# The two mix stages in written order: one stretch of attention per round, one share of dense products behind it

## The chip, the core and the metric

The kernel runs on one core of a Trainium2 chip. The metric is the device time of one execution in microseconds: the median of several runs. Beside it there is one execution that was taken with the hardware profiler; all rows below come from that one.

## What is computed

Two transformer blocks over 512 positions of width 1024, in fp32. The first block has dilated, banded and stick-breaking attention and a convolutional feed-forward part; the change doesn't touch it. The second block puts 16 meta tokens ahead (528 positions) and has two layers of: feed-forward, **mix**, feed-forward. The mix is what is changed:

```python
proj = rmsnorm(h, mix_norm[l]) @ w_in[l]
rq, rk, rv, rg, dq, dk, dv = split(proj)
y_ret = retention_group(rq, rk, rv, rg, ret_gn_w[l])        # 4 heads of 128
y_diff = diff_attention_group(dq, dk, dv, ...)              # 4 heads, two maps of 64 each
h = h + concatenate([y_ret, y_diff], -1) @ w_out[l]

# differential attention, for each head and each block of queries:
s = einsum('mid,mjd->mij', qb, k) * scale                   # two maps m, causal
p = softmax(s)
o = (p[0] - lam * p[1]) @ v                                 # then rms norm of o and a factor

# retention, for each head (written out over all positions in the kernel):
o = ((q @ k.T) * decay) @ v                                 # then group norm, times silu(gate)
```

## The kernel before

All activations lie feature-major: partitions are features, columns are positions (528, the meta tokens first). A dense product W.T y is done in fp32r with both operands split into a high and a low part, H and L, so that each tile of 128 features costs three products, HH, HL and LH (`gemm_steps`, L195 to L210, all its products on L205). One **dense step** is one k of `gemm_steps`: 128 rows, three products, over two column segments of 264 (R2, all 528 positions), so six products; over R1 (512 positions, layer 1's queries and gates) three products of 512 columns. A `gemm` of 128 output features has 8 steps. Weights come in blocks of 256 output features through `wblock` (L188): two loads of 512 KB on SP's queue into `wraw` (three buffers), a high part on ScalarE (L171) and a low part on VectorE (L172) into `wqH` and `wqL` (four buffers each, so two blocks).

The kernel is written as a program order for a planner. The planner orders the instructions of each engine by priority (the place in the program) and by what it expects to be ready, so dense products of later parts can slip in where an earlier part would wait. In a region under `manual_schedule(engines={nc.tensor.engine})` TensorE keeps the order in which its instructions are written; the other engines are ordered by the planner as elsewhere. Before, the attention of the first block is under it, the mix is not.

`mix` (L1398) does for each layer, in program order: V of the four differential heads (`v_heads`, `v_major`); for two pairs of heads the projections q and k, rotated (`rotate`) and split by `stack`, and then `diff_heads`; V of the retention heads; for two pairs of heads q and k rotated and `ret_head`; the norm of the differential outputs and their transposes (`feature_major`); the gates; the norm of the retention outputs, their transposes and products with the gates; the first half of the output projection (`w_out2a`); and the second half in halves of the columns, which also prepares the next feed-forward part.

`diff_block` (L1633) handles one head and one block b of queries. Block 0 is the 16 meta tokens (layer 0 alone); blocks 1 to 4 have 128 queries and 16 + 128 b keys. It is a generator with three visits. The first does the scores of both maps, one after the other: a product over 128 rows (L1648: `stack` has put the high part of the 64 query features over the low part, against the high part of the keys twice), a product over 64 rows (L1649: high part of q, low part of k) and, on the diagonal, a mask through a bf16 product with the identity (L1651); then the maximum on VectorE (L1653), the exponential with its sum on ScalarE (L1660), and the combination of the two maps on VectorE (L1668, L1671). 528 keys are done in two spans of 264. The second visit transposes the weights of the 128-wide key blocks (L1678) and copies them (L1679). The third transposes the 16 meta columns (L1682), copies them (L1683) and does the value products (L1685; L1686 for the 16 meta rows; fp32, so two instructions for a product). `diff_heads` (L1615) calls the visits as a pipeline: scores of block i, transposes of i-1, values of i-2.

`ret_head` (L1691) does one head of retention: scores of key block j against all later queries (L1706), times the decay (L1707, into one tile `rw`), then the value products of query block i (L1715), a copy (L1717) and the statistics (L1719, L1720).

PSUM has eight buffers: four `g` (dense products), two `s` (scores, transposes of outputs), one `t` and one `o`.

## Time and profile before

| | us |
|---|---|
| median of 3 runs | 3121.83 |
| lowest, highest | 3114.48, 3124.24 |
| the profiled execution | 3116.68 |
| its span, first to last instruction | 3114.9 |
| mix of layer 0 in it | about 1425 to 1722 |
| mix of layer 1 in it | about 2456 to 2737 |

Times in the rows are microseconds from the start of the span unless a column says ns. PE is TensorE, PEld its weight loads, DVE VectorE, ACT ScalarE, POOL GpSimd, SP the engine whose queue issues the loads. The recorded end of a product is modelled and overlaps the next product; what a product takes away from the engine is read from its start to the next start.

### The profile page before, as it was taken

The page shows a single profiled execution, that of the slowest core. Times are in us where ns is not written, and L with a number is a line of the kernel's source. Part 1 is how long each engine was busy: PE and PEld are TensorE (multiplying, and loading weights), DVE is VectorE, ACT ScalarE, POOL GpSimd, SP SyncE. Part 2 cuts the span into 40 slices and gives each one's busy share as a digit, 9 for nine tenths or more (in the row PEclk, how much of TensorE's full clock was granted, in tenths as well). Part 3 has the DMA queues.
Part 4 walks back from the last instruction along what each step waited for, and adds up shares of the span by engine and source line. Part 5 has one row for each costly group of instructions (what it writes and reads, how often), then busy time and mean ns, then how long its engine had stood idle before and what let it go on. Part 6 is the DMA issues. An engine that isn't in the chain of part 4 may idle for free.

```text
span 3114.9 us, 54477 instructions
## 1 busy us (share of the span) xinstructions
PE 3071.9 (99%) x22120; PEld 2843.6 (91%) x22120; DVE 2229.0 (72%) x4185; ACT 1522.3 (49%) x2948; POOL 30.9 (1%) x64
## 2 busy tenths in 40 slices
PE   8998999999999999999999999999999999999998
PEld 6875789998989999999899999999999988899998
DVE  5253767978877887776766877768777586687775
ACT  5445556655555554444643544444444464354443
POOL 1100100000000000000000000000000000000000
PEclk9998999999999999999999999999999999999999
DMA  6221346223323322332112232322323211223232
GB/s 222 63 85 61 105 146 200 90 95 102 109 95 113 119 89 91 100 115 90 52 58 76 76 108 89 108 93 87 109 90 114 97 58 62 72 84 106 95 109 75
DMA packets 97020, 304.38 MB, mean 98 GB/s; under 512 B 12263, under 2 KB 20863, under 8 KB 96640
## 3 DMA queue, kind: packets, MB, share of 16 engines
q1 hardware_dynamic: 90448, 286.63, 27.9%
q0 software_dynamic: 2720, 7.78, 0.8%
q10 hardware_dynamic: 3600, 6.49, 0.7%
q8 instruction: 173, 2.83, 0.4%
q14 instruction: 79, 0.65, 0.1%
HBM read 290.34 MB, written 14.45 MB: 98 GB/s over the span
## 4 chain that ended last, share of the span: by engine, by line
PE 96%; DVE 1%; ACT 1%; DMA 1%; issue 1%; DVEq 0%; SPq 0%; ACTq 0%
PE ps_g L205 37%; PE ps_g L315 18%; PE ps_g L313 9%; PE ps_s L205 8%; PE ps_g L243 7%; PE ps_o L313 4%; PE ps_g L652 1%; PE ps_o L243 1%; PE ps_s L1649 1%; PE ps_s L1706 1%; PE ps_o L1685 1%; PE ps_o L1715 1%; DMA num<-in_x 1%; PE ps_o L1686 0%; PE ps_s L1648 0%
## 5 line engine op out<-in xcount | busy, mean ns | idle before, releaser
L172 DVE TENSOR_TENSOR wqL<-wraw,wqH 128x512 fp32r<-128x512 f32 (+1 forms) x672 | 604.0, 913 | 277.4 <-ACT wqH L171 269.2
L171 ACT CAST wqH<-wraw 128x512 fp32r<-128x512 f32 (+1 forms) x672 | 526.1, 799 | 511.2 <-PE ps_g L205 278.1
L205 PE MATMUL ps_g<-yH,wqH 128*128 128x264 f32 (+2 forms) x1584 | 462.5, 329 | 0.0
L205 PE MATMUL ps_g<-yL,wqH 128*128 128x264 f32 (+2 forms) x1584 | 453.4, 322 | 0.4 <-DVE yL L451 0.4
L205 PE MATMUL ps_g<-yH,wqL 128*128 128x264 f32 (+2 forms) x1584 | 452.9, 323 | 0.3 <-DVE wqL L172 0.2
L315 PE MATMUL ps_g<-t,wqH 128*128 128x264 f32 (+1 forms) x1696 | 314.7, 283 | 0.0
L205 PEld LDWEIGHTS ps_g<-yH,wqH 128*128 128x128 f32 x1584 | 275.2, 189 | 34.0 <-issue 12.2
L205 PEld LDWEIGHTS ps_g<-yL,wqH 128*128 128x128 f32 x1584 | 276.8, 189 | 21.7 <-DVE yL L451 1.1
L205 PEld LDWEIGHTS ps_g<-yH,wqL 128*128 128x128 f32 x1584 | 274.9, 189 | 23.5 <-DVE wqL L172 0.7
L315 PEld LDWEIGHTS ps_g<-t,wqH 128*128 128x128 f32 x1696 | 262.5, 188 | 1.8
L315 PE MATMUL ps_g<-t,wqL 128*128 128x264 f32 (+1 forms) x848 | 239.5, 282 | 0.0
L171 ACT CAST wqH<-ws 128x1024 fp32r<-128x1024 f32 x96 | 101.0, 1052 | 122.7 <-issue 32.7
L315 PEld LDWEIGHTS ps_g<-t,wqL 128*128 128x128 f32 x848 | 159.9, 189 | 0.0
L313 PE MATMUL ps_g<-t,wqH 128*128 128x264 f32 (+1 forms) x768 | 142.8, 283 | 0.0
L205 PE MATMUL ps_s<-hL,wqH 128*128 128x264 f32 (+1 forms) x544 | 141.3, 317 | 0.0
L205 PE MATMUL ps_g<-hL,wqH 128*128 128x264 f32 (+1 forms) x544 | 141.2, 317 | 0.0
L205 PE MATMUL ps_g<-hH,wqL 128*128 128x264 f32 (+1 forms) x544 | 141.1, 317 | 0.0
L205 PE MATMUL ps_s<-hH,wqL 128*128 128x264 f32 (+1 forms) x544 | 141.1, 317 | 0.0
L205 PE MATMUL ps_g<-hH,wqH 128*128 128x264 f32 (+1 forms) x544 | 141.0, 317 | 0.0
L205 PE MATMUL ps_s<-hH,wqH 128*128 128x264 f32 (+1 forms) x544 | 141.0, 316 | 0.0
L295 DVE TENSOR_TENSOR ws<-wraw 128x512 f32<-128x512 f32 x96 | 66.4, 692 | 82.1 <-DMA wraw<-in_ffn_w_gate 32.6
L172 DVE TENSOR_TENSOR wqL<-ws,wqH 128x1024 fp32r<-128x1024 f32 x96 | 117.3, 1222 | 5.8 <-ACT wqH L171 1.9
(451 smaller groups left out, 8046.9 us busy)
## 6 DMA issues: line engine op xcount, KB each, us to landing
wraw<-in_ffn_w_gate SPq DMA_DIRECT2D x88, 512.0 KB, 3.7
wraw<-in_ffn_w_up SPq DMA_DIRECT2D x88, 512.0 KB, 3.7
wraw<-in_ffn_w_down SPq DMA_DIRECT2D x88, 512.0 KB, 3.5
wraw<-in_w_in SPq DMA_DIRECT2D x86, 512.0 KB, 3.7
wraw<-in_w_up SPq DMA_DIRECT2D x64, 512.0 KB, 3.7
wraw<-in_w_down SPq DMA_DIRECT2D x32, 512.0 KB, 3.6
wraw<-in_w_gate SPq DMA_DIRECT2D x24, 512.0 KB, 3.8
tmp_p<-gates ACTq DMA_DIRECT2D x24, 256.0 KB, 3.3
```

Of the source, the lines that this page charges most:

```text
L171: self.nc.scalar.copy(out=H, in_=raw)
L172: self.nc.vector.tensor_sub(out=L, in0=raw, in1=H.bitcast(F32))
L205: self.nc.tensor.matmul(t[:, :m], lhsT=a, rhs=b[:, o:o + m], start=(k == 0 and i == 0), stop=(k == nk - 1 and i == 2))
L243: self.nc.tensor.matmul(q[:, :m], lhsT=a, rhs=b[:, o:o + m], start=(k == 0 and i == 0), stop=(k == nk - 1 and i == 2))
L295: nc.vector.tensor_add(out=S[:, :512], in0=A21, in1=A22)
L313: nc.tensor.matmul(ps, lhsT=a, rhs=b, start=first, stop=last)
L315: nc.tensor.matmul(ps, lhsT=a, rhs=b, start=False, stop=last, skip_group_check=True)
L652: nc.tensor.matmul(ps[:, :256], lhsT=a[:, ts], rhs=w, start=(k == 0 and i == 0), stop=(k == KD - 1 and i == 2))
L1649: nc.tensor.matmul(ps[:nq, :e - a], lhsT=qm[r], rhs=k[2][r, a:e], start=False, stop=not dg)
L1685: nc.tensor.matmul(ops[:nq, :P], lhsT=aT[:, j * P:j * P + nq], rhs=V[:, j], start=(j == 0), stop=False)
L1706: nc.tensor.matmul(ps[:cnt, :e - a], lhsT=k[:, j * P:j * P + cnt], rhs=q[:, a:e], start=True, stop=True)
L1715: nc.tensor.matmul(ops[r0:n, :P], lhsT=w[:cnt, off[j] + i0 + r0:off[j] + i0 + n], rhs=V[:cnt, j], start=(j == 0), stop=(j == i))
```

## The change

The whole mix from the first attention on is put under `manual_schedule` for TensorE, and its parts become generators that are woven together by hand. `mingle(main, side)` takes a stretch of `main`, which says how many steps of `side` follow it; `shares` gives the pipeline of the attention n rounds and divides 32 dense steps among them. What goes with what:

- differential heads 0 and 1, with the values of retention (they stood behind the differential attention before)
- q and k of differential heads 2 and 3, alone
- differential heads 2 and 3, with q and k of retention heads 0 and 1
- the scaling of the differential outputs; then retention heads 0 and 1, six rounds each, with q and k of retention heads 2 and 3
- retention heads 2 and 3, with the gates and the transposes of the differential outputs
- the norm and transposes of the retention outputs, with `w_out2a`

Weight blocks are asked for in the new order, one ahead. `stack` gives way to `parts`: high and low part of all 128 rows at once, the scale already in q. `diff_block` does the scores as three rounds of two 64-row products, one per map, in the two halves of the rows; 528 keys are done as 512 and 16. The 16 meta columns are transposed as a full 128-column block against rows of V that are set to zero on POOL, so that the value product is over 128 rows (block 0 alone keeps 16). The two maps are combined in one wide pass, and the division by the first map's sum moves to the copy of the output. Buffers: `qk2` 10 to 14, `vh` 6 to 8 (retention's outputs share them), `rot` 3 to 2, `P` 4 to 6 (retention's weighted scores use three of them instead of `rw`). The old `pipeline` of three stretches per step is kept for the first block as `pipeline3`.

The core of the diff; lines that go away are left out where the printed functions show them.

```diff
+def mingle(main, side):
+    for n in main:
+        for _ in range(n):
+            next(side, None)
+
+def shares(steps, n, total):
+    for i in range(n):
+        next(steps)
+        yield (i + 1) * total // n - i * total // n
+    drain(steps)
...
+    def pipeline(self, steps):
+        last = todo = None
+        for step in steps:
+            next(step)
+            if todo:
+                next(todo)
             if last:
                 next(last, None)
             yield
             last, todo = todo, step
         next(todo)
         if last:
             next(last, None)
         yield
         next(todo, None)
...
     def mix(self, l, R):
+            order = [2, 3, 6, 7, 4, 5, 8, 9, 10, 11, 12, 13]
+            blocks = {i: w for i, w in enumerate(self.pre)}
+            def wi(i):
+                for j in order[:2] if i not in order else order[:order.index(i) + 2]:
+                    if j not in blocks:
+                        blocks[j] = self.wblock(A["w_in2"][l, j], KD, step=1024)
+                return blocks[i]
...
+            nb = 5 if R.off == 0 else 4
...
+            def queries(i0, use):
+                out = []
+                for j in range(2):
+                    for n in range(2):
+                        ps = yield from self.gemm_steps(wi(i0 + j), n, ys, (R, R2)[j] if use == "diff" else R2)
+                        if self.vlate:
+                            self.vlate()
+                            self.vlate = None
+                        if use == "diff":
+                            out.append(self.parts(self.rotate(ps, rot, True), (R, R2)[j], None if j else SCALE))
+                        else:
+                            out.append(self.rotate(ps, rot, False))
+                self.qk = out[:2], out[2:]
...
+            def gates():
+                out = diff_out()
+                for i in (12, 13):
+                    for n in range(2):
+                        if sg:
+                            next(out)
+                        g = self.tmp("sg", 4)
+                        self.evac_mul(g, (yield from self.gemm_steps(wi(i), n, ys, R)), rb)
+                        nc.scalar.activation(out=g[:, s], in_=g[:, s], func=AF.Silu)
+                        sg.append(g)
+                drain(out)
...
+            def ret_out():
+                rc = self.rsqrt_small(rst[:, :, :, 1], 1.0, 1.0)
+                for h in range(4):
+                    o, p = ro[h], sg[h]
...
+                    yield 8 if h == 0 else 4
...
+            drain(values(0, NMETA, V))
+            rot = self.rot_tables("rope", rb)
+            drain(queries(2, "diff"))
+            n = 2 * nb + 1
+            with self.tc.manual_schedule(engines={nc.tensor.engine}):
+                side = values(6, 0, U)
+                mingle(shares(diff(0), n, 32), side)
+                drain(side)
+                drain(queries(4, "diff"))
+                rot = self.rot_tables("ret", rb)
+                main, side = diff(2), queries(8, "ret")
+                mingle(shares(main, n, 32), side)
+                drain(side)
+                diff_scale()
+                main, side = retain(0), queries(10, "ret")
+                mingle(main, side)
+                drain(side)
+                main, side = retain(2), gates()
+                mingle(main, side)
+                drain(side)
+                side = out_a()
+                mingle(ret_out(), side)
+                drain(side)
...
-    def stack(self, t, R, key):
+    def parts(self, t, R, scale=None):
+        H, L = [self.tmp("qk2", 14, dt=F32R) for _ in range(2)]
+        self.split(t, H, L, R.off, R.n, scale)
+        return H, L
...
     def v_major(self, vT, c0):
-        out = self.qp.tile([P, 5, P], F32, name="vh", tag="vh", bufs=6)
+        out = self.qp.tile([P, 5, P], F32, name="vh", tag="vh", bufs=8)
+        nc.gpsimd.memset(out[:, 4], 0.0)
...
     def diff_block(self, b, lam, q, k, V, o_sb, oss):
+        spans = [(0, nk)] if nk <= 512 else [(NMETA, nk), (0, NMETA)]
...
+        for i, (a, e) in enumerate(spans):
+            ps = [self.psum("sg"[i])[:nq, :e - a] for _ in range(2)]
+            for j, (x, y) in enumerate(((0, 0), (1, 0), (0, 1))):
+                for m in range(2):
+                    nc.tensor.matmul(ps[m], lhsT=q[x][r[m], qs], rhs=k[y][r[m], a:e], start=(j == 0),
+                                     stop=(j == 2 and i == 1))
+            if i == 0:
+                for m in range(2):
+                    nc.tensor.matmul(ps[m][:, e - a - nq:], lhsT=self.identb[:nq, :nq], rhs=self.dm[:nq, :nq],
+                                     start=False, stop=True)
+            pst.append(ps)
+        for i, ps in enumerate(pst):
+            for m in range(2):
+                c = 2 * i + m
+                nc.vector.tensor_reduce(out=sm[:nq, c:c + 1], in_=ps[m], axis=AX.X, op=ALU.max, negate=True)
+        if len(spans) == 2:
+            nc.vector.tensor_tensor(out=sm[:nq, 0:2], in0=sm[:nq, 0:2], in1=sm[:nq, 2:4], op=ALU.min)
+        Pm = [self.tmp("P", 6) for _ in range(2)]
         for m in range(2):
             for i, (a, e) in enumerate(spans):
+                c = 4 + 2 * i + m
+                nc.scalar.activation(out=Pm[m][:nq, a:e], in_=pst[i][m], func=AF.Exp, bias=sm[:nq, m:m + 1],
+                                     accum_out=sm[:nq, c:c + 1])
+        if len(spans) == 2:
+            nc.vector.tensor_add(out=sm[:nq, 4:6], in0=sm[:nq, 4:6], in1=sm[:nq, 6:8])
+        nc.vector.reciprocal(out=sm[:nq, 8:10], in_=sm[:nq, 4:6])
+        nc.vector.scalar_tensor_tensor(out=sm[:nq, 10:11], in0=sm[:nq, 4:5], scalar=sm[:nq, 9:10], in1=lam[:nq],
+                                       op0=ALU.mult, op1=ALU.mult)
         a = Pm[0]
+        nc.vector.scalar_tensor_tensor(out=a[:nq, :nk], in0=Pm[1][:nq, :nk], scalar=sm[:nq, 10:11], in1=a[:nq, :nk],
+                                       op0=ALU.mult, op1=ALU.add)
         yield
...
+                nc.tensor.transpose(pt[:, j * P:(j + 1) * P], a[:, NMETA + j * P:NMETA + (j + 1) * P], self.ident)
+            if b < 4:
+                nc.tensor.transpose(pt[:, b * P:(b + 1) * P], a[:, :P], self.ident)
+            else:
+                pm = self.psum("g")
+                nc.tensor.transpose(pm[:, :P], a[:, :P], self.ident)
+                nc.scalar.copy(out=aT[:, 4 * P:], in_=pm[:, :P])
...
         yield
         ops = self.psum("o")
+        m = slice(b * P, b * P + nq)
+        if b == 0:
+            nc.tensor.transpose(ops[:16, P:P + nq], a[:nq, :16], self.ident[:nq, :nq])
+            nc.scalar.copy(out=aT[:16, m], in_=ops[:16, P:P + nq])
         for j in range(b):
+            nc.tensor.matmul(ops[:nq, :P], lhsT=aT[:, j * P:(j + 1) * P], rhs=V[:, j], start=(j == 0), stop=False)
+        kk = 16 if b == 0 else P
+        nc.tensor.matmul(ops[:nq, :P], lhsT=aT[:kk, m], rhs=V[:kk, 4], start=(b == 0), stop=True)
+        nc.vector.tensor_scalar(out=o_sb[:nq, b], in0=ops[:nq, :P], scalar1=sm[:nq, 8:9], scalar2=None, op0=ALU.mult)
...
     def ret_head(self, h, q, k, V, R, o_sb, rst):
+        w3 = [self.tmp("P", 6) for _ in range(3)]
...
+            if j in (0, 2, 4):
+                yield 3
...
+            if i in (1, 2, 4):
+                yield (2, 2, 3)[(1, 2, 4).index(i)]
```

## Rows read from the trace of the kernel before

**Rows 1.** The page's first part: each engine's busy time, share of the span, instructions.

```profile
PE 3071.9 (99%) x22120; PEld 2843.6 (91%) x22120; DVE 2229.0 (72%) x4185; ACT 1522.3 (49%) x2948; POOL 30.9 (1%) x64
```

**Rows 2.** Stages: length; PE, PEld, DVE, ACT, POOL busy; granted clock, DMA share, GB/s.

```profile
1425.00:1722.00 297.00, 296.67 (x2237) 270.48 (x2236) 196.74 (x534) 138.26 (x356) 0.00 (x0) 1.00 0.21 68
2456.00:2737.00 281.00, 280.89 (x1856) 243.50 (x1855) 185.16 (x466) 129.38 (x316) 0.00 (x0) 1.00 0.22 72
1476.00:1580.00 104.00, 103.67 (x695) 85.10 (x695) 79.66 (x262) 62.89 (x207) 0.00 (x0) 1.00 0.14 49
```

**Rows 3.** Timeline of TensorE in layer 0's mix: start, duration, engine, line, operation.

```profile
1499.61 0.28 PE L205 MATMUL ps_g<-yH,wqH 128*128 128x264 f32 x1
1499.73 0.28 PE L1648 MATMUL ps_s<-tmp_qk,tmp_qk 128*128 128x264 f32 x1
1499.94 0.38 PE L1649 MATMUL ps_s<-tmp_qk,tmp_qk 64*128 64x264 f32 x1
1500.26 0.23 PE L1651 MATMUL ps_s<-dm,identb 128*128 128x128 bf16 x1
1500.30 0.37 PE L205 MATMUL ps_g<-yH,wqH 128*128 128x264 f32 x1
1500.50 0.83 PE L1685 MATMUL ps_o<-vh,tmp_aT 128*128 128x128 f32 x6
1501.26 0.48 PE L1686 MATMUL ps_o<-vh,tmp_aT 16*128 16x128 f32 x2
1501.67 0.51 PE L205 MATMUL ps_g<-yL,wqH 128*128 128x264 f32 x2
```

**Rows 4.** Timeline of TensorE in block 1's stick-breaking attention, under `manual_schedule`.

```profile
276.99 0.40 PE L205 MATMUL ps_g<-yH,wqL 128*128 128x512 f32 x1
277.32 0.70 PE L1065 MATMUL ps_s<-qk 64*128 64x256 f32 x4
277.95 0.29 PE L1067 MATMUL ps_s<-cm,identb 128*128 128x128 bf16 x2
278.05 0.47 PE L205 MATMUL ps_g<-yH,wqH 128*128 128x512 f32 x1
278.36 0.39 PE L205 MATMUL ps_g<-yL,wqH 128*128 128x512 f32 x1
...
240.91 1.50 PE L1065 MATMUL ps_s<-qk 64*128 64x512 f32 x4
242.34 0.29 PE L1067 MATMUL ps_s<-cm,identb 128*128 128x128 bf16 x2
```

**Rows 5.** VectorE's groups, 1425 to 1740: busy us, mean ns, idle before.

```profile
L172 DVE TENSOR_TENSOR wqL<-wraw,wqH 128x1024 fp32r<-128x1024 f32 x28 | 34.2, 1220 | 14.0 <-ACT wqH L171 14.0
L1653 DVE TENSOR_REDUCE sm<-ps_s 128x1 f32<-128x264 f32 x16 | 6.9, 431 | 7.3 <-PE ps_s L1651 3.9 <-PE ps_s L1649 3.4
L1653 DVE TENSOR_REDUCE sm<-ps_s 128x1 f32<-128x400 f32 x8 | 4.6, 571 | 1.8 <-PE ps_s L1651 1.7
L1671 DVE SCALAR_TENSOR_TENSOR tmp_P<-tmp_P,sm 128x528 f32<-128x528 f32 x4 | 3.0, 758 | 0.0
L1667 DVE RECIPROCAL sm<-sm 128x1 f32<-128x1 f32 x16 | 2.5, 154 | 0.9 <-ACT tmp_P L1660 0.7
L1458 DVE TENSOR_SCALAR od<-od,sd 128x128 f32<-128x128 f32 x16 | 3.4, 269 | 0.0
```

**Rows 6.** ScalarE's groups of exponentials in the same stretch.

```profile
L1660 ACT ACTIVATE tmp_P<-ps_s,sm 128x264 f32<-128x264 f32 x16 | 7.5, 473 | 5.2 <-DVE sm L1658 5.1
L1660 ACT ACTIVATE tmp_P<-ps_s,sm 128x400 f32<-128x400 f32 x8 | 4.7, 586 | 1.4 <-DVE sm L1666 1.4
```

**Rows 7.** Table by stage around a wait in block 1; columns as in rows 2.

```profile
231.00:234.00 3.00, 0.81 (x6) 0.40 (x5) 1.94 (x3) 2.05 (x3) 0.00 (x0) 1.00 0.00 0
234.00:238.00 4.00, 3.67 (x13) 2.22 (x13) 1.26 (x6) 0.94 (x5) 0.00 (x0) 0.57 0.59 197
```

**Rows 8.** The page's part on loads: count, size, median us from issue to landing.

```profile
wraw<-in_w_in SPq DMA_DIRECT2D x86, 512.0 KB, 3.7
```

238 lines of the change are left out of this document (79 added, 159 removed).

## The prediction

> **What bounds the kernel now.** I read the page first: TensorE is busy for 99% of the span [rows 1]. So time is won only by giving TensorE less to do, and lost wherever it is made to wait. Next comes the table by stage for the two mix stages, the only ones that the change touches [rows 2]: TensorE is busy for 296.67 of 297.00 us in layer 0 and for 280.89 of 281.00 in layer 1, while VectorE is at about 66%. In the attention part of layer 0 (the third row) VectorE is at 77%. The order that the planner made has practically no wait in it, so nothing is to be won by filling gaps. Busy is not the same as working well, though. That shows in the timeline of TensorE, read from start to start [rows 3]. A dense product of 264 columns takes 0.12 us. The score product over 128 rows behind it takes 0.21, the one over 64 rows 0.32, the mask 0.04, and the dense product behind that 0.20. At 2.4 GHz, 264 columns are 0.11. So each time the engine goes from 128 rows to 64 and back it loses about 0.3 us, and 0.08 more on its return to dense work. The value products show the same for 16 rows: six of 128 rows take 0.76 (five of 0.11 and a last one of 0.20), the two of 16 rows 0.41.
>
> **The change, part by part.**
>
> *Scores.* Before, each map and key span is a group of its own. Its price from [rows 3]: 0.31 of overhead, twice nk columns at 2.4 GHz, 0.04 of mask, 0.08 of return. With 144, 272 and 400 keys that is 0.55, 0.66 and 0.76; with 528 keys in two spans 1.26. Times two maps: 1.10, 1.32, 1.52, 2.52. Block 0 (16 keys, layer 0 alone) has no row: between 0.62 and 0.86, say 0.8. A head costs 7.3 us in layer 0 and 6.5 in layer 1; four of each make 55.
>
> After, three pairs of 64-row products follow each other, and the two maps lie in the two halves of the rows. The nearest row is stick-breaking in block 1, which has the same form: 64-row pairs, then two masks, then dense [rows 4]. Four products of 256 columns, each 0.213 us (fp32 moves at half rate here, as 0.11 for 128 columns in [rows 3] shows), take 0.63 instead of 0.85 one after another: two run at a time (0.43), plus 0.20. The dense product ahead takes 0.33 where 512 columns need about 0.23, the masks 0.10, the dense product behind 0.31. Overhead of one visit: 0.10 + 0.20 + 0.10 + 0.08 = 0.48. A pair then costs nk columns at 2.4 GHz; for 144 and fewer, where a product may wait for its weights, I take 0.11, the 128-row value product's spacing in [rows 3] (0.06 at best, which would save some 2 more in all). Blocks 1 to 3: 0.81, 0.82, 0.98. Block 4: 0.48 + 3 x 0.213 = 1.12, and its 16 keys 3 x 0.11 + 0.30, together 1.75. Block 0: 0.5 to 0.85, say 0.65. A head costs 5.0 and 4.4; four of each 37.5. Saved: 17.4.
>
> One row speaks against the 512-column pairs: the same group with 512 columns takes 1.43 us [rows 4], where 2 x 0.43 + 0.20 would be 1.06. By it each of the eight blocks 4 loses about 0.28, 2.3 in all; the 256-column row loses nothing. Those rows are fp32, the new products fp32r, so I take half: 16.3 saved. (The Trainium skill, "TensorE: Matmul & The Clock Gate", part 3, says that products in different row groups run together, some 4 ns apart; its example has 512 columns. The 256-column row agrees, the 512-column row doesn't. By the page alone the saving would be 17.4.)
>
> *Value products and transposes.* The 16 meta keys get a full 128-row product (zero rows in V) instead of a 16-row one. Before: 0.09 too much on the last 128-row product, 0.41, and some 0.1 on the return; after: 0.22. 0.38 saved in each of 32 blocks with index 1 to 4, 12.2 us. The full transpose that replaces a 16-column one costs 0.11 more or less what the 16-column one cost with its return: nothing.
>
> *Off TensorE.* Gone are one wide VectorE pass per block, and half of what `stack` did: `parts` splits 128 rows at once. VectorE isn't the bound, so this is worth nothing by itself; it lightens the queue for the chain below. The zeroing of V on POOL (8 a layer) meets an engine that is at 1% [rows 1], and V is read rounds later: nothing.
>
> *Moved loads.* SP's queue gets the weight blocks in a new order (retention's values before the second pair of attention heads) and one block ahead. A load lands in 3.7 us [rows 8], a block has at least 32 dense products of 0.12 on each of six operands, over 11 us: hidden. The retention tables now wait for the last use of the rotary ones (two buffers for three), but have all of a dense stretch for it.
>
> So TensorE's own work falls by 16.3 + 12.2 = **28.5 us** (24 with the 512-column row in full and the worse block 0, 32 with the better ends).
>
> *The wait that is added.* The written order is binding for TensorE. A round is: scores of block i, transposes of i-1, values of i-2, then a share of dense steps (six products, 0.73 us each; 32 steps over 11 rounds, over 9 in layer 1). If the softmax of i-1 is late, everything behind its transposes waits, dense work too, and nobody else can go ahead. The softmax chain of block 4, from the start of its first mask: 0.25 to reach VectorE; two maxima of 512 keys, 0.69 each by the slope between 264 and 400 [rows 5], overlapping to 1.3; two short ones and the minimum, 0.4; four exponentials, 0.68 by the slope in [rows 6] and some 0.27, 1.9; sum, reciprocal, factor at 0.15; the wide combination 0.76 [rows 5]; with some 0.1 for each hand-over about 5.7 us. TensorE gets to its transposes after 0.7 (16-key group) + 0.44 + 0.67 + 2.3 + 0.7 = 4.8 us, behind the last block of a call after 4.1. It waits 0.9 and 1.6 us; layer 1 with shares of four steps 0 and 0.9. Two calls per layer: 6.8. Blocks 1 to 3 have chains of 2.4, 2.9, 3.4 against 4.0, 3.7 and 4.3: no wait if nothing is in the way.
>
> Something will be: one weight split holds VectorE for 1.22 us [rows 5]. I add 0.45 for each block 4, 3.5 in all (nothing if the chain always goes first; 1.2 at each block 2 to 4 gives 17). Block 0 of layer 0 transposes, copies and multiplies in one visit, with no work between: about 0.8 four times, 3.2. The 20 scalings of `od`, now ahead of retention's first multiplications, are 5.4 us of VectorE [rows 5] while two score buffers carry TensorE for some 3: 1 a layer, 2 (0 to 5). The first scores behind a dense stretch wait for `parts` of the last key: 1.5 in all (0 to 5). Sum of the waits: **17 us** (9 to 37).
>
> **Sum.** -28.5 + 17 = -11.5. The profiled execution took 3116.68 us, span 3114.9 and 1.8 around it; so 3105 for such a one. It lies 5 us under the median of the three runs, 3121.83, and I take the difference to the median: **3110 us**, 0.4% faster. A measurement of this kernel can tell about 0.3% from no change, that is 9.4 us.
>
> **The rivals.**
> - *The chain always goes first, block 0 is covered.* Waits of 5 us: about 3097. For it: VectorE loses a wide pass in each block, and the third row of [rows 2] still has 23% free. Against it: even alone, blocks 4 are late by the sum above.
> - *Given back.* An operation of 1.2 us stands in the way of every block 2 to 4: waits near 30, 3122, no change.
> - *Slower.* The softmax chain becomes the bound of the attention rounds: one long operation on VectorE and one on ScalarE are in each chain of blocks 2 to 4. Blocks 4 then wait 3.5 us, blocks 3 and 2 1.2 to 1.4: eight heads 49, with the rest 55: 3148. It decides from 38 us of waits, 1.3 in each of 24 such blocks and what stands beside. Waits of that length can cost the clock as well: behind a stretch of 3 us in which TensorE was busy for 0.81, the granted clock was 0.57 in the next 4, the lower of its two levels for most of it [rows 7], 1.7 us lost; at eight blocks 4 that is 14 more. (The skill's page named above, in "Why this matters for your kernels", warns of just such gaps; the row agrees.) Against it: VectorE would have to be far busier than 77%, and the change makes it less busy.
> - *The pairs don't run together in fp32r.* Three more pairs' worth of columns per block, 2.1 us per head, 17 in all: 3127. [Rows 4] show the overlap in fp32, nothing shows it in fp32r.
>
> **Chances.** Forecast (3103 to 3117) 0.46, first rival 0.20, given back 0.17, slower 0.12, no pairs 0.05. About 0.7 of the forecast's lies under 3112.5: faster 0.53. Same 0.34: the rest of it, given back, no pairs. Slower 0.13. The range goes from a little below the first rival to the edge of slower, 3092 to 3130.
>
> **What would show it.** In the profile after: pairs of 64-row products 0.01 us apart, no 16-row value products but for block 0, the stretch of layer 0's mix near 294 us instead of 297, layer 1's near 272 instead of 281; waits of TensorE almost all on transposes of block 4 (`tmp_P` from VectorE), 1 to 2.5 us each, with none on dense products. Waits at blocks 2 and 3 as well mean the third or second rival; a granted clock under 1 in the mix the third; starts of a pair 0.1 us apart the fourth. Wrong most easily: the share of the waits, whose contended part rests on the planner's order of VectorE, which no row of before shows.

## The result, and the profile after

The changed kernel takes **3149.29 us** (median of 4 runs, 3145.05 to 3152.64), the kernel before 3119.66 beside it: a ratio of 1.0095, with an interval from 1.0071 to 1.0118. It is slower by 0.9%; forecast were 3110 us and a range up to 3130. The profiled execution has a span of 3150.8 us, 35.9 more than before.

The page's line on the engines:

```profile
PE 3063.4 (97%) x22208; PEld 2844.6 (90%) x22208; DVE 2202.2 (70%) x4045; ACT 1504.7 (48%) x2896; POOL 33.4 (1%) x80
```

And the table by stage, for both mix stages and for layer 0's second pair of attention heads (columns as in rows 2):

```profile
1428.00:1735.00 307.00, 279.82 (x2184) 259.12 (x2184) 176.14 (x442) 123.56 (x320) 1.23 (x8) 0.97 0.19 63
2481.00:2767.00 286.00, 269.15 (x1853) 238.87 (x1852) 169.30 (x395) 118.32 (x284) 1.23 (x8) 0.96 0.21 68
1549.00:1625.00 76.00, 64.33 (x495) 57.57 (x493) 47.03 (x116) 37.36 (x114) 0.00 (x0) 0.93 0.19 62
```

Beside [rows 1] and [rows 2] three things are new. TensorE, which was never idle in these stages, now is for 27 of 307 and 17 of 286 us. Its granted clock is 0.97 and 0.96 instead of 1.00. And VectorE is *less* busy: 57% of layer 0's stage where it was 66%, and 62% in the third row, an attention stretch. So TensorE waits for a VectorE that has time to spare.

What it waits for, layer 0 first, then layer 1 (us in total, times, longest):

```profile
PE ps_t L1743 <- DVE tmp_P L1736: 8.7, 3, 3.7
PE ps_o L1761 <- ACT tmp_aT L1757: 4.8, 4, 1.4
PE ps_s L1711 <- ACT tmp_P L1728: 3.4, 4, 1.2
PE ps_t L1743 <- DVE sm L1732: 2.9, 2, 1.5
PE ps_o L1787 <- DVE tmp_qk L1527: 2.7, 2, 2.1
PE ps_s L1777 <- DVE tmp_P L1778: 1.8, 2, 1.7
...
PE ps_t L1743 <- DVE tmp_P L1736: 7.0, 5, 2.4
PE ps_s L1711 <- ACT tmp_P L1728: 5.3, 4, 1.9
PE ps_s L1777 <- DVE tmp_P L1778: 1.1, 2, 0.9
```

L1743 are the transposes, which wait for the softmax chain (L1721 to L1736). L1761 is block 0's value product behind its own transpose and copy. L1711 are scores, whose two buffers are free only when the exponentials (L1728) of the block before have read them. L1787 and L1777 are retention.

To compare all kernels below, I take one stretch from each profile: from the first product of `lam` to the last one of `out_a`, in both layers. It shows the sum of both lengths, TensorE's idle time in them (length less busy time), and the granted clock in each layer.

The ratios are to runs of the kernel before beside each (medians 3115.83 to 3119.66).

| kernel | median us | ratio to before | mix stretches, us | TensorE idle, us | clock, layers 0 and 1 |
|---|---|---|---|---|---|
| before | 3119.66 | 1 | 555.5 | 0.4 | 1.00, 1.00 |
| changed | 3149.29 | 1.0095 | 587.8 | 44.0 | 0.97, 0.96 |
| `planner` | 3099.44 | 0.9944 [0.9923, 0.9965] | 533.6 | 3.7 | 1.00, 1.00 |
| `attention_free` | 3107.92 | 0.9972 [0.9956, 0.9987] | 544.7 | 11.9 | 1.00, 1.00 |
| `scores_alone` | 3189.95 | 1.0233 [1.0213, 1.0253] | 621.9 | 34.1 | 0.87, 0.92 |
| `scores_o` | 3110.92 | 0.9982 [0.9972, 0.9992] | 554.5 | 3.1 | 0.98, 1.00 |
| `order_alone` | 3249.15 | 1.0432 [1.0413, 1.0450] | 679.0 | 70.0 | 0.91, 0.90 |
| `rot_early` | 3143.47 | 1.0092 [1.0075, 1.0109] | 581.9 | 39.4 | 0.97, 0.98 |
| `b0_visit` | 3142.51 | 1.0075 [1.0055, 1.0094] | 579.3 | 39.6 | 0.97, 0.98 |
| `block4_work` | 3145.97 | 1.0091 [1.0069, 1.0113] | 581.0 | 38.0 | 0.96, 0.97 |
| `warm` | 3152.37 | 1.0105 [1.0077, 1.0133] | 586.8 | 34.7 | 0.97, 0.97 |
| `dense_between` | 3122.22 | 1.0016 [1.0006, 1.0026] | 561.5 | 27.5 | 0.99, 0.98 |
| `written_three` | 3122.81 | 1.0017 [1.0005, 1.0029] | 559.9 | 24.2 | 0.99, 0.98 |
| `planner_plus` | 3096.40 | 0.9927 [0.9912, 0.9942] | 531.3 | 3.6 | 1.00, 1.00 |

Of the 35.9 us that the span grew, 32.3 lie in these stretches. One profile of a kernel moves them by some 3 us from case to case: `b0_visit` changes nothing in layer 1, whose stretch is 2.8 us shorter there all the same. Outside the stretches executions differ as well: in the profile of `planner` TensorE runs at half its clock from 215 to 239 us, in block 1, which the change doesn't touch, and its first stretch starts 9.3 us later than that of the kernel before. So I read differences of a few us from the stretches and not from the medians.

### The profile page after: what moved, and what is told of

Same layout as the page of the kernel before. It is cut to its first block, busy times and chain, and to the rows that moved or that the text cites. A ratio compares the mean times of both kernels' runs of the same rounds, so it can differ in the third digit from the quotient of the medians.

```text
span 3150.8 us, 54454 instructions
## 1 busy us (share of the span) xinstructions
PE 3063.4 (97%) x22208; PEld 2844.6 (90%) x22208; DVE 2202.2 (70%) x4045; ACT 1504.7 (48%) x2896; POOL 33.4 (1%) x80
## 4 chain that ended last, share of the span: by engine, by line
PE 90%; DVE 4%; ACT 3%; DMA 2%; issue 1%; DVEq 0%; SPq 0%; ACTq 0%
PE ps_g L220 35%; PE ps_g L330 17%; PE ps_g L328 9%; PE ps_s L220 8%; PE ps_g L258 7%; PE ps_o L328 4%; PE ps_g L684 1%; PE ps_o L258 1%; DMA tmp_p<-gates 1%; ACT tmp_P L1728 1%; DVE wqL L187 1%; PE ps_o L1787 1%; ACT wqH L186 1%; PE ps_s L1711 1%; DMA num<-in_x 0%
## 5 line engine op out<-in xcount | busy, mean ns | idle before, releaser
L220 PE MATMUL ps_g<-yH,wqH 128*128 128x264 f32 (+2 forms) x1584 | 469.9, 336 | 0.0
L220 PE MATMUL ps_g<-yH,wqL 128*128 128x264 f32 (+2 forms) x1584 | 451.4, 324 | 0.3 <-DVE wqL L187 0.2
L220 PE MATMUL ps_g<-yL,wqH 128*128 128x264 f32 (+2 forms) x1584 | 449.3, 322 | 0.4 <-DVE yL L466 0.4
L220 PEld LDWEIGHTS ps_g<-yH,wqH 128*128 128x128 f32 x1584 | 278.7, 193 | 38.1 <-issue 16.5
L220 PEld LDWEIGHTS ps_g<-yH,wqL 128*128 128x128 f32 x1584 | 278.7, 192 | 22.1 <-DVE wqL L187 0.7
L220 PEld LDWEIGHTS ps_g<-yL,wqH 128*128 128x128 f32 x1584 | 279.4, 192 | 19.8 <-DVE yL L466 1.1
L186 ACT CAST wqH<-ws 128x1024 fp32r<-128x1024 f32 x96 | 101.0, 1052 | 122.8 <-issue 34.7
L220 PE MATMUL ps_s<-hL,wqH 128*128 128x264 f32 (+1 forms) x544 | 141.2, 317 | 0.0
L220 PE MATMUL ps_g<-hL,wqH 128*128 128x264 f32 (+1 forms) x544 | 141.1, 317 | 0.0
L220 PE MATMUL ps_g<-hH,wqL 128*128 128x264 f32 (+1 forms) x544 | 141.0, 317 | 0.0
L220 PE MATMUL ps_s<-hH,wqL 128*128 128x264 f32 (+1 forms) x544 | 141.0, 317 | 0.0
L220 PE MATMUL ps_g<-hH,wqH 128*128 128x264 f32 (+1 forms) x544 | 141.0, 316 | 0.0
L220 PE MATMUL ps_s<-hH,wqH 128*128 128x264 f32 (+1 forms) x544 | 140.9, 316 | 0.0
```

Of the source, the lines that this page charges most:

```text
L186: self.nc.scalar.copy(out=H, in_=raw)
L220: self.nc.tensor.matmul(t[:, :m], lhsT=a, rhs=b[:, o:o + m], start=(k == 0 and i == 0), stop=(k == nk - 1 and i == 2))
```

## The experiments

My theory after the result: the new products are as cheap as forecast; the loss is that TensorE follows the written order while the softmax chain, behind other work in VectorE's and ScalarE's queues, is late, and that its clock falls behind the longer waits. The rival: the new products, or the new form of the softmax, cost the time themselves.

### Who orders TensorE: `planner` and `attention_free`

```diff
-            with self.tc.manual_schedule(engines={nc.tensor.engine}):
+            if True:
```

> The changed kernel, but the planner orders TensorE's work in the mix, too, as it did before the change; what is written there only says in which order the work comes to the planner. My theory: the changed products save about 29 us, as forecast, and the whole loss, some 46 us of waits and 17 us at the lower clock, comes from TensorE having to follow the written order while the softmax chain is late. Then the waits and the drops of the clock go away: about 3091 us, 58 less than the changed kernel. Rival: the waits come from the work itself (the chain is too long for what other work there is, whoever orders it), and the planner finds no more to put in than what is written: 3130 to 3149. Second rival: the order in which work comes to the planner costs as much as a binding order: the same range, but with waits at other places.

3099.44 us: 50 less than the changed kernel, 0.6% below the kernel before. The two stretches:

```profile
1434.99:1706.72 271.73, 270.73 (x2165) 251.06 (x2164) 172.83 (x438) 121.46 (x318) 1.23 (x8) 1.00 0.23 71
2455.47:2717.33 261.86, 259.17 (x1829) 230.44 (x1828) 166.05 (x390) 117.00 (x282) 1.23 (x8) 1.00 0.23 73
```

The work is that of the changed kernel, with no wait to speak of and the full clock. That divides the result. TensorE is busy here for 529.9 us, before for 555.1: products and sequence of the change, ordered by the planner, save **25.2**. The changed kernel is busy for 543.8 with the same work: **13.9** more, most of it at the lower clock. And it is idle for 44.0 where the kernel before is for 0.4: **43.6**. Together -25.2 + 13.9 + 43.6 = +32.3, the growth of the stretches.

`attention_free` lets the planner order the attention rounds only; from the scaling of the attention outputs on the order stays written:

```diff
-            with self.tc.manual_schedule(engines={nc.tensor.engine}):
+            if True:
                 side = values(6, 0, U)
...
+            with self.tc.manual_schedule(engines={nc.tensor.engine}):
                 diff_scale()
```

> The changed kernel, with TensorE's order bound to the written one only from the scaling of the attention outputs on (retention, gates, first output product); the attention rounds with their dense products are ordered by the planner. This splits the 50 us that the planner's order won in all. My theory: the attention rounds hold 33 to 36 of the 46 us of waits and nearly all of the lower clock: 3103 to 3112 us. Rival: the retention rounds hold as much as the attention ones (the order of retention in six rounds is new, too): 3120 to 3130.

3107.92 us: 41 of the 50 us lie in the attention rounds, and the whole of the lower clock. Retention and the last rounds hold the other 9: 11.9 us idle where `planner` has 3.7, and TensorE busy for 532.8 us where it is for 529.9 there, both without a fall of the clock. So of the 13.9 some 11 to 14 are the clock's.

### Products without order, order without products: `scores_alone`, `scores_o`, `order_alone`

`scores_alone` is the kernel before with `diff_block`, `parts` and `v_major` of the changed one; heads come one after another, and the planner orders. Its calls in `mix`:

```diff
-                q = [self.stack(self.rotate(self.gemm(wq, n, ys, R), rot, True), R, False) for n in range(2)]
+                q = [self.parts(self.rotate(self.gemm(wq, n, ys, R), rot, True), R, SCALE) for n in range(2)]
...
-                k = [self.stack(self.rotate(self.gemm(wk, n, ys, R2), rot, True), R2, True) for n in range(2)]
+                k = [self.parts(self.rotate(self.gemm(wk, n, ys, R2), rot, True), R2) for n in range(2)]
```

> The kernel before with the products of the change alone: pairs of 64-row scores, masks, the 128-row product for the 16 meta keys, one split for both maps and the shorter softmax; the order is the planner's and the heads come one after another as before. My theory: TensorE's work falls by 28 to 30 us and no wait comes in: 3089 to 3094 us, 0.9% below the kernel before. Rival: the new softmax form brings waits of its own (all four score buffers of a block are held until the last exponential): between 3100 and 3120. If the pairs don't run together: about 3107.

3189.95 us, 72 more than before: by itself, with these buffers, the cheaper form is a large loss, and all my numbers are wrong. TensorE's groups in the attention stretch of layer 0, 1486 to 1604 us (count, busy us, mean ns, idle before):

```profile
L1640 PE MATMUL ps_s<-tmp_qk,tmp_qk 64*128 64x144 f32 (+4 forms) x114 | 31.0, 454 | 10.3 <-ACT tmp_P L1657 10.3
L1688 PE MATMUL ps_o<-vh,tmp_aT 128*128 128x128 f32 x72 | 20.0, 428 | 2.0 <-DVE sm L1652 1.6 <-ACT tmp_aT L1680 0.4
L205 PE MATMUL ps_g<-yH,wqH 128*128 128x264 f32 x66 | 14.2, 297 | 0.0
L205 PE MATMUL ps_g<-yL,wqH 128*128 128x264 f32 x66 | 13.8, 291 | 0.0
L205 PE MATMUL ps_g<-yH,wqL 128*128 128x264 f32 x64 | 13.2, 286 | 0.0
```

The same stretch in the table by stage:

```profile
1486.00:1604.00 118.00, 100.57 (x536) 81.11 (x537) 62.14 (x174) 48.97 (x179) 0.41 (x2) 0.66 0.09 29
```

The planner put in 196 dense products (66 + 66 + 64), the kernel before had 391 in its 104 us. With so little between, TensorE waits for the exponentials, and the granted clock is 0.66. Why so few? Block 4 takes two of the four `g` buffers for its 16-key scores and one for a transpose. The dense products behind come later in the program and get their `g` buffers in turn, so after block 4. `scores_o` takes that bond away (its edit against `scores_alone`):

```diff
-            ps = [self.psum("sg"[i])[:nq, :e - a] for _ in range(2)]
+            if i == 0:
+                ps = [self.psum("s")[:nq, :e - a] for _ in range(2)]
+            else:
+                ps = [self.psum("ot"[m])[:nq, :16] for m in range(2)]
...
-                pm = self.psum("g")
+                pm = self.psum("o")
```

> The kernel before with the products of the change, as in the run of the new products alone, but block 4's score products of the 16 meta keys and their transpose use the buffers of the value products and transposes, not two of the four buffers of the dense products. In the run of the new products alone TensorE had half the dense products of the kernel before in its attention stretch (196 of them for 391) and fell to the lower clock. My theory: those dense products come later in the program and get their buffers in turn, behind block 4's; without that bond the planner pulls dense work between the attention blocks as before: 3095 to 3115 us. Rival: the pair of score buffers that each block holds until its last exponential is what starves TensorE, and dense work was not pulled for another reason: 3160 to 3190.

3110.92 us, 79 less, within what the theory gave: idle time falls from 34.1 to 3.1 us, and 465 dense products stand in 1486 to 1600. It doesn't reach `planner`: 12 us are missing by the medians, 20.9 by the stretches. Up to 7 us of that are a fall of the clock in layer 0 (0.94 over the 116 us from 1484 to 1600). The rest is not waits but work: in layer 1, at the full clock, TensorE is busy for 268.5 us where in `planner` it is for 259.2. Most of that lies in the scores, in whether the two maps' products stand beside each other. `planner`'s timeline of layer 1 has both cases, one map alone (three products and its mask) and both in turn (six and two):

```profile
2510.42 0.64 PE L1711 MATMUL ps_s<-tmp_qk,tmp_qk 64*128 64x272 f32 x3
2510.99 0.23 PE L1715 MATMUL ps_s<-dm,identb 128*128 128x128 bf16 x1
...
2528.71 0.64 PE L1711 MATMUL ps_s<-tmp_qk,tmp_qk 64*128 64x272 f32 x6
2529.28 0.28 PE L1715 MATMUL ps_s<-dm,identb 128*128 128x128 bf16 x2
```

Either takes 0.57 us to its mask, so one map alone costs as much as both. Of the 132 pairs of both layers 120 start within 20 ns of each other in the changed kernel, 98 in `planner` and 36 in `scores_o`. Summed from start to start, scores and masks of layer 1 take 24.7 us before, 17.5 in `planner` and 23.2 in `scores_o`: the form pays where the order keeps the pairs together. Another 2.9 us in layer 1 are retention's products, which `scores_o` has in the old form.

`order_alone` is the reverse: the written order with the old `diff_block`, `stack` and `v_major`:

```diff
-                            out.append(self.parts(self.rotate(ps, rot, True), (R, R2)[j], None if j else SCALE))
+                            out.append(self.stack(self.rotate(ps, rot, True), (R, R2)[j], bool(j)))
```

> The changed kernel with the products and the softmax of the kernel before: only the written order, the rounds and the moved loads of the change. My theory: TensorE does the 29 us of work again that the new products saved, and waits at least as long as in the changed kernel, since each block's chain has one wide pass more on VectorE and TensorE a little more to do meanwhile: waits of 40 to 60 us and 15 to 25 us at the lower clock, 3175 to 3200 us. Rival: the waits come from the new softmax form (the maxima of both maps after all products of the block): then the old form, which starts the first map's maximum while the second is still being multiplied, waits little: 3120 to 3140.

3249.15 us, beyond either number. The waits of layer 0:

```profile
PE ps_s L1719 <- ACT tmp_P L1731: 16.0, 8, 4.1
PE ps_o L1756 <- ACT tmp_aT L1754: 12.0, 16, 1.1
```

With the old form a block 4 needs the two `s` buffers twice, so its second map's scores wait for the first map's exponentials inside the visit (in the timeline 4 of the 8 waits, 1.5 to 2.2 us each; the other four, up to 4.1, are block 1's scores behind a dense stretch). The 16-row copy stands in front of every block's value products (16 times). In a bound order nobody passes them. So the new form belongs to the written order: it takes 100 us of waits, lower clock and work out of it. It is the order that doesn't pay.

### One wait at a time: `rot_early`, `b0_visit`, `block4_work`, `warm`

The longest wait of the changed kernel is 3.73 us, from 1567.48 to 1571.21. SyncE's queue ahead of it (start, duration, engine, line, operation, count):

```profile
1564.08 2.08 SPq L1639 DMA_DIRECT2D rot<-in_ret  x2
```

And VectorE's timeline (the same, with the idle time before):

```profile
1566.24 0.71 DVE L373 TENSOR_TENSOR tmp_qk<-tmp_sg,tmp_qk 128x528 fp32r<-128x528 f32 x1 [0.21 <-ACT tmp_qk L372]
1568.67 0.71 DVE L1640 TENSOR_TENSOR rot<-rot,tmp_rb 128x528 f32<-128x528 f32 x1 [1.72 <-DMA rot<-in_ret]
1569.29 0.16 DVE L1732 RECIPROCAL sm<-sm 128x2 f32<-128x2 f32 x1
1569.37 0.42 DVE L1721 TENSOR_REDUCE sm<-ps_s 128x1 f32<-128x272 f32 x1
```

The retention tables are asked for at 1564.08, when the last key of the dense stretch has read the rotary ones. Their multiplication stands on VectorE ahead of the reciprocal and the maxima of the first attention blocks, and VectorE holds still for 1.72 us with those behind it. `rot_early` asks before that dense stretch (queries and keys then have 13 buffers instead of 14, to make room):

```diff
-            t = self.qp.tile([P, TT], F32, name="rot", tag="rot", bufs=2)
+            t = self.qp.tile([P, TT], F32, name="rot", tag="rot", bufs=4)
...
+                rot2 = self.rot_tables("ret", rb)
                 drain(queries(4, "diff"))
-                rot = self.rot_tables("ret", rb)
+                rot = rot2
```

> The changed kernel with four buffers for the tables of the rotations instead of two, and the retention tables asked for, and multiplied on VectorE, ahead of the second stretch of queries and keys (13 buffers instead of 14 for queries and keys make the room). In the changed kernel VectorE stands 1.72 us at that multiplication, waiting for its transfer, with the softmax chain of the first block queued behind it; TensorE then waits 3.73 us in layer 0 and 2.38 in layer 1, and its clock falls behind the first of these. My theory: these two waits shrink by 5 us and one drop of the clock of 3 us goes: 3139 to 3144 us. Rival: VectorE's queue is full there anyway (splits of the last keys) and the chain is as late without the transfer: 3147 to 3150.

3143.47 us, 6 less by the medians and in the theory's range. The ratio to the kernel before, 1.0092 for 1.0095, can't tell it from the changed kernel, though, and that of the next three can't either; what each edit does is read from the waits. Here: 4.6 us less idle, the longest wait at the transposes 2.8 in layer 0, 1.8 in layer 1. The fall of the clock behind it didn't go, though; layer 0 still shows 0.97.

`b0_visit` gives block 0 its transpose and copy one visit earlier:

```diff
+        else:
+            pt = self.psum("t")
+            nc.tensor.transpose(pt[:16, :nq], a[:nq, :16], self.ident[:nq, :nq])
+            nc.scalar.copy(out=aT[:16, :nq], in_=pt[:16, :nq])
         yield
...
-        if b == 0:
-            nc.tensor.transpose(ops[:16, P:P + nq], a[:nq, :16], self.ident[:nq, :nq])
-            nc.scalar.copy(out=aT[:16, m], in_=ops[:16, P:P + nq])
```

> The changed kernel with block 0's transpose and its copy in the second of the block's three visits, as for the other blocks, not in the third with the value product right behind it. My theory: the four waits of 1.2 to 1.4 us in layer 0 for that copy go, some 5 us: 3143 to 3146 us, and in the profile no wait of the value product for the copy is left. Rival: TensorE then waits for block 0's softmax in the second visit instead: 3148 to 3152.

3142.51 us, 7 less by the medians, and no wait for the copy is left. Layer 0's stretch is 5.7 us shorter; the new transpose waits twice for the softmax instead (4.1 us), both times behind a dense stretch, so the rival holds for those two blocks.

`block4_work` moves dense steps of the same call to where the longest chain is:

```diff
-        yield (i + 1) * total // n - i * total // n
+        k = 7 if i in (n // 2 - 1, n - 2) else 0
+        rest = total - 14
+        j = i - (i > n // 2 - 1) - (i > n - 2)
+        yield k or (j + 1) * rest // (n - 2) - j * rest // (n - 2)
```

> The changed kernel with other shares of the same 32 dense steps: 7 behind the scores of each block 4 (whose softmax chain is the longest), 2 or 3 behind each other block, where it was 2 or 3 in layer 0 and 3 or 4 in layer 1 everywhere. My theory: the waits are the length of the chain less the work between a block's scores and its transposes. Then the transposes of block 4, and the scores behind them, which wait for some 15.7 us in all, wait for under 4, the others up to 3 more, and some of the lower clock goes with them: 3128 to 3138 us. Rival: the chain is late because VectorE and ScalarE have other work queued ahead of it; more dense steps bring more of that work, and the wait stays: 3145 to 3152.

3145.97 us: the rival's number by neither cause. What is left of the waits at L1746 (the transposes, L1743 before), in layer 0 and in layer 1, beside the new ones:

```profile
PE ps_t L1746 <- DVE tmp_P L1739: 2.8, 1, 2.8
PE ps_g L223 <- ACT tmp_P L1731: 1.7, 2, 1.1
...
PE ps_s L1714 <- ACT tmp_P L1731: 7.3, 6, 2.6
PE ps_t L1746 <- DVE tmp_P L1739: 2.9, 1, 2.9
PE ps_g L223 <- ACT tmp_P L1731: 2.6, 4, 1.1
```

All eight waits of block 4's transposes are gone; the two rows left are the table's. So their price was the chain less the work between, as the prediction worked it out. But the seven dense steps now wait themselves (L223, 4.3 us): the 16-key scores hold two of their four `g` buffers until the exponentials. And scores elsewhere wait longer (L1714 in layer 1, 7.3 for 5.3).

`warm` asks about the clock: useless transposes of the identity in front of those of block 4, 12 in layer 0 and 8 in layer 1.

```diff
+            for j in range((12 if self.warm else 8) if b == 4 else 0):
+                nc.tensor.transpose(pt[:, :P], self.ident, self.ident)
```

> The changed kernel with useless work on TensorE ahead of the transposes of each block 4: 12 transposes of the identity (8 in layer 1), about 1.3 and 0.9 us, where TensorE waits for 1.5 to 2.8 and 0.7 to 1.8 us; they are written over by the real ones. No wait gets shorter for the rest, but TensorE is idle for some 9 us less. My theory: the lower clock (about 17 us lost) follows from these idle times and those around them; with them filled, several of the ten drops in the mix stages go: 3137 to 3146 us. Rival: the drops come from the form of the work (64-row products, products of 16 rows) and not from idle time: the same drops, and the time stays or grows by up to 3 us: 3148 to 3153.

3152.37 us. TensorE is idle for 9.3 us less, the stretch is 1.0 shorter, and there are eight falls of the clock, as many as in the changed kernel. The changed kernel's table around the first of its eight (columns as in rows 2):

```profile
1485.00:1488.40 3.40, 1.98 (x18) 1.31 (x17) 2.10 (x8) 1.48 (x7) 0.00 (x0) 1.00 0.00 0
1488.40:1491.80 3.40, 3.40 (x18) 3.16 (x18) 0.60 (x3) 0.27 (x2) 0.00 (x0) 0.50 0.00 0
```

TensorE was busy for 1.98 of 3.40 us, and in the next 3.40 it runs at the lower of its two levels, 1.2 GHz, although it is busy all the time. The idle piece is block 0's copy (1.42 us), not block 4's transposes, which `warm` filled. So block 4's waits weren't the ones that brought the clock down: in the changed kernel, too, none of the eight falls stands behind one. That idle time does it at all is only in part borne out. `planner`, `attention_free` and the kernel before have no fall in the mix, but `attention_free` is idle for 11.9 us. Around block 4's longest wait, 2.81 us, the changed kernel kept its clock; and in `scores_o` it fell where TensorE was hardly idle, behind 10.2 us with only seven dense products among 64:

```profile
1613.00:1617.00 4.00, 1.19 (x11) 1.01 (x11) 1.94 (x5) 2.86 (x10) 0.00 (x0) 1.00 0.00 0
1617.00:1621.00 4.00, 4.00 (x37) 4.00 (x36) 0.86 (x2) 2.03 (x5) 0.00 (x0) 1.00 0.36 131
...
1544.60:1554.80 10.20, 10.10 (x64) 7.37 (x65) 6.17 (x23) 6.79 (x25) 0.00 (x0) 1.00 0.00 1
1554.80:1568.40 13.60, 13.60 (x53) 11.35 (x53) 5.36 (x13) 4.68 (x16) 0.00 (x0) 0.50 0.13 40
```

So the rival, that the form of the work has a part in it, isn't settled. The places also move from kernel to kernel (`rot_early` has nine falls, `b0_visit` seven), so single waits can't be priced from these runs.

### More work between: `dense_between` and `written_three`

Still a written order, but the dense share stands between the scores of block i and the transposes of block i-1. From a block's scores to its transposes there are then two shares instead of one.

```diff
             next(step)
+            yield
             if todo:
                 next(todo)
             if last:
                 next(last, None)
-            yield
             last, todo = todo, step
+        yield
         next(todo)
         if last:
             next(last, None)
-        yield
         next(todo, None)
```

> The changed kernel with the dense share of each attention round moved: behind the scores of block i and ahead of the transposes of block i-1, where it was behind the values of block i-2. TensorE's order is still bound to the written one. Between a block's scores and its transposes there are then two dense shares instead of one, some 2.2 us more. My theory: TensorE waits because the softmax chain, with the splits queued ahead of it on VectorE and ScalarE, is longer than the work written between; 2.2 us more cover all waits at transposes of block 4 and of the first blocks of a call but the one for the retention tables, which falls from 3.7 to some 1.5 us; the waits of block 0 stay: 3128 to 3138 us. Rival: the score buffers are now the limit (a block's two are free only after its exponentials, and scores of the next come two dense shares later anyway), or the dense steps bring their own splits and the chain gets later by as much: 3143 to 3150.

3122.22 us, 27 less than the changed kernel and better than the theory's range. Idle time falls from 44.0 to 27.5 us, the falls of the clock from eight to four. The waits that stood for most of the loss, in layer 0:

```profile
PE ps_o L1761 <- ACT tmp_aT L1757: 2.2, 4, 0.7
PE ps_s L1711 <- ACT tmp_P L1728: 2.0, 2, 1.2
PE ps_t L1743 <- DVE tmp_P L1736: 1.7, 3, 1.0
```

The transposes wait for 1.7 us where they waited for 11.6, the table's wait among them is down from 3.7 to 1.0, and block 0's copy comes at half the price. Moving the `yield` is worth more than the first three edits above together (6, 7 and 3 us by the medians).

`written_three` adds the edits of `b0_visit` and `rot_early`.

> Three edits at once, still in written order: the dense share between scores and transposes, block 0's transpose in the second visit, and the retention tables early with four buffers. My theory: what the three remove adds up (some 15, 6 and 6 us): 3118 to 3127 us, and in the attention rounds neither a wait over 1 us nor the lower clock; what is left above the planner's order (3099) is retention and the last rounds. Rival: the waits replace one another, and the three together give no more than the largest of them: 3133 to 3142.

3122.81 us: in the theory's range, but not by its working. The two other edits add nothing that can be measured (the stretches are 1.6 us shorter): the second share had already covered what they take away. Left are retention, the ends of the calls, and scores waiting for exponentials (5.3 us in layer 1).

### A version faster than both: `planner_plus`

`planner` with the edits of `b0_visit` and `rot_early`.

> The changed kernel with the mix in the planner's order from start to end, block 0's transpose in the second visit, and the retention tables early with four buffers. My theory: the planner already finds work for nearly all of these waits (3.3 us were left in both layers), so this gives 0 to 3 us more than the planner's order alone: 3096 to 3100 us. Rival: tighter buffers (13 for queries and keys) and the earlier transpose bind the planner more than they help: 3101 to 3106.

**3096.40 us**, a ratio of 0.9927 to the kernel before. Beside `planner` the gain is 3 us, within the spread of either; the 0.7% to the kernel before are not.

## Why the prediction was wrong

**The work: the sum right, in part by luck.** 28.5 us were forecast, 24 to 32 by the bounds; TensorE's busy time fell by 25.2 (`planner`) to 27.4 (`planner_plus`: 527.7). By parts, summed from start to start over both stretches, `planner` against before: scores with masks 14.0 less (16.3 forecast), the attention's value products 10.8 less (12.2), its transposes 3.5 more, which I had put at nothing. That is 21.3, under my lower bound. Retention's products, which weren't in my sum, gave another 5.0 (44.0 us for 49.0). The scores fall short because the planner breaks up some pairs: in `dense_between`, a bound order, they take 17.9 less. The step that I split in half, the 512-column pairs, had nearly the full gain. TensorE's timeline after (rows of an attention visit):

```profile
1495.59 0.96 PE L1711 MATMUL ps_s<-tmp_qk,tmp_qk 64*128 64x512 f32 x6
1496.49 0.29 PE L1715 MATMUL ps_s<-dm,identb 128*128 128x128 bf16 x2
1496.70 0.50 PE L1711 MATMUL ps_g<-tmp_qk,tmp_qk 64*128 64x16 f32 x6
```

Six products of 512 columns, three pairs, take 0.90 us from start to start. Three times 512 columns at 2.4 GHz are 0.64, and the 0.26 beside them is little more than the 0.20 that I had allowed. So the fp32 row with 1.43 us [rows 4] didn't bear on fp32r. (The rule of the Trainium skill, "TensorE: Matmul & The Clock Gate", part 3, that pairs in different row groups run together, holds here at 512 columns too.) The rival "no pairs" falls for the changed kernel; in `scores_o`, where the order parts them, its price shows.

**The waits: 17 forecast, 43.6 measured.** Term by term, from the rows of waits and the single waits in the timeline of TensorE:

| term | forecast | measured |
|---|---|---|
| transposes of block 4, with contention | 10.3 | 12.5, and 1.5 at the scores behind them |
| block 0, copy in the same visit | 3.2 | 4.8 |
| scalings of `od` and retention's products with the decay | 2 | 2.9 |
| first blocks behind a dense stretch | 1.5 | 7.2 |
| retention tables | 0, "hidden" | 6.1 (3.73 and 2.38) |
| V's transposes and retention's values, for the `o` buffer | not listed | 4.5 |

Together 39.5; most of the rest, 3.2, are the first output products, which wait for the last transposed differential outputs (L220 for L1526 and L1527), not listed either. Block 4's chain, on which most of the working went, is nearly right. What failed are the steps that I passed over in a sentence. The tables "have all of a dense stretch": wrong end of it. With two buffers for three the request waits for the *last* reader, which is the last key of that stretch, so it starts where the stretch is over; and it isn't TensorE that waits for the load but VectorE, with the chain behind it. The first blocks of a call I put at 1.5 in all: a weight split and the last key's shuffle, two products, sum and split stand on VectorE in front of or between the first block's steps. From layer 1's timeline, TensorE's mask of the first block and then VectorE:

```profile
2531.71 0.29 PE L1715 MATMUL ps_s<-dm,identb 128*128 128x128 bf16 x2
...
2532.21 1.23 DVE L187 TENSOR_TENSOR wqL<-wraw,wqH 128x1024 fp32r<-128x1024 f32 x1 [1.05 <-ACT wqH L186]
...
2533.36 0.75 DVE L1653 STREAM_SHUFFLE tmp_t<-tmp_t 128x528 f32<-128x528 f32 x1
2534.01 0.75 DVE L1659 TENSOR_TENSOR tmp_sg<-ps_g,rot 128x264 f32<-128x264 f32 x2
2534.68 0.70 DVE L1660 TENSOR_TENSOR tmp_t<-tmp_t,rot 128x528 f32<-128x528 f32 x1
2535.30 0.30 DVE L1721 TENSOR_REDUCE sm<-ps_s 128x1 f32<-128x144 f32 x1
2535.51 0.69 DVE L1661 TENSOR_TENSOR tmp_sg<-tmp_sg,tmp_t 128x528 f32<-128x528 f32 x1
2536.13 0.30 DVE L1721 TENSOR_REDUCE sm<-ps_s 128x1 f32<-128x144 f32 x1
```

The two maxima take 0.3 us each and could start at about 2532.0 (the 0.25 us behind the first mask that I had allowed). The first starts at 2535.30, behind 1.2 us of weight split and 1.9 of rotation, the second behind 0.6 more.

**The clock: 0 forecast, some 11 to 14 measured.** The only row that I had for it [rows 7] I used in the rival alone, with 1.7 us for each wait. The eight falls come to 1.4 to 1.7 each, but that they agree is luck: they last from 3.4 to 10.2 us, 41 in all at 1.2 GHz. And the place was wrong: I tied the price to waits of 3 us at blocks 4; no fall stands behind one of those, and three of the eight stand behind block 0's copy, 1.42 us. (The Trainium skill, "TensorE: Matmul & The Clock Gate", "Why this matters for your kernels", warns of idle gaps longer than that; the rows here show falls behind shorter gaps, and in `scores_o` one behind hardly any, and they decide.) Without the clock, the forecast with the waits as they were would have been 3121.83 - 25 + 44 = 3141.

**The rival "slower"** had 3148, and 3149 came, by luck: its mechanism is not what happened. It made the chain a bound through VectorE's load and I gave it little chance because VectorE would have to be busier than 77%. VectorE was at 62%. The share of an engine's busy time says how much work it can take, not how soon it gets to one instruction; in a bound order the second counts. What was late was each chain's position in a queue. `dense_between` shows it from the other side: same work on every engine, one share more between, and the transposes' waits in both layers fall from 18.6 us to 5.6 (2.4 at L1743 and 3.2 at block 4's last one, L1748, which hardly waited before).

**The comparison itself** rested on a true reading ("the order that the planner made has practically no wait in it"), from which I should have asked what a bound order can win over that: at most its 0.4 us of idle time. `planner` answers it: the bound order takes 50 us back. The written sequence is worth something all the same, as what the planner is given: `scores_o`, the new attention products in the old sequence, gains 6 us (at most 13 without its fall of the clock), `planner` 18.

Open stays which waits, or which work, bring the clock down, and why the planner keeps the pairs together in one sequence and parts them in the other.

## What to carry to other kernels

An order written by hand for one engine needs, between a step and the step that reads its result through other engines, enough work for the *whole* queue in between, not for the chain alone: here one share left TensorE idle for 44 us, two for 27, and the planner's order for 4. When a buffer is shared by fewer tables, look for the last reader, and for who stands behind the instruction that waits for the load. Price a wait of TensorE with its clock: here 44 us of idle time came with 41 us at the lower clock, which cost some 11 to 14, though the 12 us of `attention_free` came with none. And a cheaper form needs its order and its buffers: the scores of layer 1 save 7.3 us where most pairs stay together and 1.5 where most are parted, and three `g` buffers taken in the wrong turn cost 79 us.

## What the runs showed of the hardware

A product of 64 rows and 272 columns for one map alone takes as long as the pair for both: three and six of them each took 0.57 us. fp32r pairs of 512 columns ran together (three in 0.90 us); the fp32 ones of [rows 4] took 1.43 for two. An idle piece of 1.42 us, with TensorE busy for 1.98 of 3.40 us around it, was followed by 3.4 us at 1.2 GHz, in which the engine was busy all the time; one of 2.81 us, with TensorE busy for 1.19 of 4.00, was not followed by a fall; and in `scores_o` 13.6 us at 1.2 GHz followed 10.2 us in which it was busy for 10.10. Transposes of the identity in eight other waits changed nothing in the number of falls. VectorE held still for 1.72 us at an instruction that waited for its load, with ready softmax steps queued behind it.
